# HGRN values of seven heads in token order: blocks by way of memory and VectorE transposes in place of TensorE transposes

## The chip, the core and the metric

The kernel runs on one core of a Trainium2 chip. The core has a matrix engine (TensorE, PE in the profile; its weight loads are PEld), a vector engine (VectorE, DVE), an engine for activations (ScalarE, ACT), GpSimd (POOL) and an engine that here only issues transfers (SyncE, SP). Each of them works through its own queue in order and waits on semaphores for the others; 16 DMA engines move the data. TensorE writes into PSUM, the other tiles lie in SBUF. The metric is the device time of one execution in microseconds (us). The kernel before takes 1769.57 us, the median of three runs (1768.42 to 1771.63).

## The reference, cut to what matters

The program is one step of a decoder layer for 1024 prompt tokens and 8 decode tokens: a norm and one input projection, an HGRN2 recurrence with 8 heads (key and value width 128) beside a Mamba-2 mixer, an output projection, and a gated MLP. The change concerns the HGRN heads, whose core is

```python
def hgrn2_chunk(S, inp):
    q, k, v, g = inp
    b = jnp.cumsum(g, axis=2)
    o = jnp.einsum('bhtk,bhkv->bhtv', q * jnp.exp(b), S)
    decay = jnp.exp(jnp.where(causal, diff, -jnp.inf))
    A = jnp.einsum('bhtsk,bhsk->bhts', decay * q[:, :, :, None, :], k)
    o = o + jnp.einsum('bhts,bhsv->bhtv', A, v)
    S_new = jnp.exp(b_last[:, :, 0])[..., None] * S + jnp.einsum('bhsk,bhsv->bhkv', k * jnp.exp(b_last - b), v)
```

Both products with v sum over the token s. On TensorE the index that is summed lies on the partitions, so v is needed with tokens on the partitions, while the projection leaves it with its 128 channels there.

## The kernel before, in words

**Jobs.** Every large product is cut into jobs; a job (`in_job`, L290) multiplies one 128-column block of a weight with the 1032 tokens in three chunks of 344, with 72 matmuls, and empties each chunk with ScalarE (L819 for the heads). Its weight is loaded by `wload` (L180): a transfer into one of two buffers `ws` (L189), a ScalarE cast into `wh` (L190, two buffers), a VectorE subtraction into `wl` (L192). `load_ahead` keeps the loads two jobs ahead. `head_in` (L807) makes the four jobs of a head: f, q, v and sg. The jobs stand in the order of the Mamba mixer's z0 to z3, head 0's four, z4 to z7, then those of heads 1 to 7, then the output projection. Along with the z jobs runs `ssm_decode` (L627), whose loads (`Bb`, `Cb`, `Sd`) also go through SP and whose arithmetic is on VectorE, ScalarE and GpSimd; each z chunk is gated on VectorE (L673, the tile `sz`), its squares are summed (`gacc`), and matmuls `ms` with the vector work of L651 to L653 and L696 finish the norm during head 0.

**Heads.** `head(h)` (L830) is a generator. `drive` (L266) takes matmuls of the coming jobs between its pieces, in proportion to the numbers that it yields; so head h runs among the matmuls of the jobs of head h+1. It begins when job sg of its own head is done. First come the transposes of the value tile `v`: one for the 8 decode tokens (`vd`, L835) and eight of 128x128 for the prompt (`vtp`, L840), with a ScalarE copy of each four into the half tiles `vt` (L841). Then L902 writes q times f over `v`. The pieces that follow compute the near products (`near`, L882, tiles `a0` to `a6`) between rounds of scaling on VectorE (`scale`, L873 and L874, with the running products `tt` of L879), then the decode states' product (`od`, copied by L944), the transposes of the keys (`ktp`), the state updates (`kv`, L965) and the outputs (`o`), where `kv` and `o` read `vt`. GpSimd's L1003 ends the head and `mix_d` stores it (L1008). The decode values go through memory as well: `vd_d` is written (L844) and read back broadcast as `vb`.

**Order.** PE's order is the program's (`manual_schedule`). The order on the other engines and on SP is set by the framework's scheduler, which places instructions by its own estimates of time; `fetch` (L172) lets a load be placed anywhere behind the last weight load, so that loads can stand ahead of work that the program has earlier.

Of the kernel before, what the change touches and what calls it, by code (L numbers as in the profile page):

```python
# [8 lines left out]
F32 = mybir.dt.float32  # L9
# [7 lines left out]
P = 128  # L17
DM = 1024
T = 1024
# [5 lines left out]
H = 8  # L25
SH = 16
CHUNK = 128
NC = T // CHUNK
# [22 lines left out]
def hybrid_layer(  # L51
# [9 lines left out]
    V, A, G, PE, SP = nc.vector, nc.scalar, nc.gpsimd, nc.tensor, nc.sync  # L61
# [5 lines left out]
    dram = ctx.enter_context(tc.tile_pool(name="dscr", bufs=1, space=DRAM))  # L67
# [3 lines left out]
    def nm(s):  # L71
        cnt[0] += 1
        return f"{s}_{cnt[0]}"
# [8 lines left out]
    def tl(tag, name, dt=F32):  # L82
        w, n = TAGS[tag]
        return (work if tag in ("hT", "big", "e", "g") else tmp).tile([P, w], dt, tag=tag, bufs=n, name=nm(name))

    def half(name):
        return tl("s", name)[:, :512]

    def bank(s, tag="mx"):
        return psmx.tile([P, 512], F32, tag=tag, bufs=NBANK[tag], name=nm(s))  # L90
# [81 lines left out]
    def fetch(dst, src):  # L172

        with tc.issue_after(last_w[0].ins):
            SP.dma_start(dst, src)
# [50 lines left out]
    def job(name, load, run):  # L226
        jobs.append((name, load, run))
# [51 lines left out]
    def w_in(off):  # L279
        return lambda: wload(w_in_[0, :, off:off + P], KT)  # L280

    def steps(w, m0, m1, hi, lo, cs, out):
        kt = len(hi)
        for k in range(kt):
            for i, (a, x) in enumerate(((w[0], hi), (w[0], lo), (w[1], hi))):
                mm(out, a[:, k, m0:m1], x[k][:, cs], start=(k == 0 and i == 0), stop=(k == kt - 1 and i == 2))
                if k < kt - 1 or i < 2:
                    yield True

    def in_job(name, off, evict, begin=None, end=None):  # L290
        def run(w):
            if begin is not None:
                begin()
            for c, cs in enumerate(chunks):
                ps = psmm.tile([P, 512], F32, tag="mm", name=nm("mm"))[:, :CH]
                yield from steps(w, 0, P, hT_hi, hT_lo, cs, ps)
                evict(c, cs, ps)
                if c == NCH - 1 and end is not None:
                    end()
                yield True  # L300
        job(name, w_in(off), run)

    def in_job_last(name, off, evict, begin):

        def run(w):
            begin()
            ps = [psmm.tile([P, 512], F32, tag="mm", name=nm("mm"))[:, :CH] for _ in chunks]
            for k in range(KT):
                for c, cs in enumerate(chunks):
                    for i, (a, x) in enumerate(((w[0], hT_hi), (w[0], hT_lo), (w[1], hT_hi))):  # L310
                        mm(ps[c], a[:, k, :], x[k][:, cs], start=(k == 0 and i == 0), stop=(k == KT - 1 and i == 2))
                        if k < KT - 1 or i < 2:
                            yield True
                    if k == KT - 1:
                        evict(c, cs, ps[c])
                        yield True
        job(name, w_in(off), run)
# [120 lines left out]
    for i in range(9):  # L438
        n = P if i < 8 else ND
# [290 lines left out]
    def once(work):  # L730
        def run():
# [19 lines left out]
    G.affine_select(eye8, eye8, pattern=[[1, ND], [-1, ND]], compare_op=ALU.is_equal, fill=0.0, base=0,  # L751
                    channel_multiplier=0)
    vd_d = dram.tile([H, ND, P], F32, name="vd_d")

    am = const.tile([P, NC, P], F32, name="am")
    G.memset(am, 0.0)
# [50 lines left out]
    def head_in(h):  # L807
        t = {}

        def f_end():  # L810
            f, k = t["f"], tl("big", "k")
            A.activation(f[:, :NT], f[:, :NT], AF.Identity, bias=lbt[:, 0, h:h + 1], scale=lbt[:, 1, h:h + 1])
            V.tensor_scalar(k[:, :NT], f[:, :NT], -1.0, 1.0, op0=ALU.mult, op1=ALU.add)
            t["k"] = k

        for n, off, func in (("f", OFF_F, AF.Sigmoid), ("q", OFF_Q, AF.Silu), ("v", OFF_I, AF.Copy),
                             ("sg", OFF_G, AF.Silu)):
            def evict(c, cs, ps, n=n, func=func):
                A.activation(t[n][:, cs], ps, func)  # L819

            def begin(n=n):
                t[n] = tl("e" if h == 0 and n == "f" else "big", n)

            if h == H - 1 and n == "sg":
                in_job_last(f"{n}{h}", off + h * P, evict, begin)
            else:
                in_job(f"{n}{h}", off + h * P, evict, begin, f_end if n == "f" else None)
        return t

    def head(h, t):  # L830
        f, k, q, v, sg = (t[n] for n in ("f", "k", "q", "v", "sg"))
# [3 lines left out]
        PE.transpose(dps[:ND, :P], v[:, T:NT], ident)  # L835
        vt = [half("vt"), half("vt")]
        for hf in range(2):
            ps = bank("vtp")
            for i in range(4):
                PE.transpose(ps[:, blk[i]], v[:, hf * 512 + i * P:hf * 512 + (i + 1) * P], ident)  # L840
            A.copy(vt[hf], ps)  # L841
# [100 lines left out]
            mm(ops[32 * g:32 * g + 32, :P], qb[:, b, :], Sds[b // 4][:, b % 4, :], start=(b < 4), stop=(b >= 4))  # L942
        odr = small.tile([P, P], F32, tag="odr", bufs=1, name=nm("odr"))
        V.tensor_copy(odr, ops[:, :P])  # L944
        yield 3.5

        for hf in range(2):
# [30 lines left out]
        for hf in range(2):  # L978
            oh = sg[:, hb[hf]]
            ps = bank("o")  # L980
            for i in range(4):
                n = hf * 4 + i
                Sb, c = before[n], slice(n * P, (n + 1) * P)
# [113 lines left out]
    heads = [None] * H  # L1097
    ssm_gate(0)
    heads[0] = head_in(0)
    ssm_gate(1)  # L1100
    heads[1] = head_in(1)
    job("conv", None, once(lambda: spread(conv_states(), 60, lambda: spread(token_blocks(), 40))))
    for h in range(2, H):
        heads[h] = head_in(h)
# [9 lines left out]
    with tc.manual_schedule(engines={mybir.EngineType.PE}):  # L1114
        finish("x3")
        drive(ssd(0), 45.5, "x7")
        drive(ssd(1), 45.5, "v0")
        finish("z7")
        for h in range(H):
            drive(head(h, heads[h]), 32.0 if h else 35.0, f"sg{h + 1}" if h < H - 1 else "o12.2")  # L1120
        finish("o12.6")
        for r0 in (0, 4):
            mixes[r0] = mix_load(r0)
# [321 lines left out]
    for c in (3, 0, 1, 2):  # L1445
# [4 lines left out]
        for t0 in range(cs.start, cs.stop, P):  # L1450
            n = min(P, cs.stop - t0)
# [49 lines left out]
```

## Time and profile before

| | |
|---|---|
| median of three runs | 1769.57 us |
| the profiled execution, and its span | 1770.87 us, 1769.2 us |
| PE busy, DVE busy | 1717.5 us (97%), 1123.7 us (64%) |
| ACT busy, POOL busy | 824.7 us (47%), 503.6 us (28%) |
| matmul of 128x344 in a job | 326 ns long, the next starts 0.16 us later |
| transposes vtp (L840) | x64, 272 ns each; first at 383.4 us, last at 823.1 us |
| first transposes vd (L835) of heads 0 and 7 | 383.3 us, 822.2 us |
| copies of vt (L841) | x16, 598 ns |
| mean DMA rate | 110 GB/s |

The profile is of one execution. A matmul's duration includes the time until its result is out, and the next one starts long before that; what an instruction costs a busy PE is therefore the step from its start to the next start. Rows of waits name the line that waits, the instruction that ended the wait, the total in us, the count and the longest. A timeline row gives start, duration, engine, line and operation, output and inputs, and in brackets the idle time before it with its cause. SPq rows are transfers being issued, not the transfers themselves.

### The profile page before, as it was taken

To read this page: it belongs to the slowest core of one execution; us is meant where nothing else is said; L and a number is where in the kernel's file an instruction comes from. 1 tells how busy PE (TensorE), PEld (TensorE's weight loads), DVE (VectorE), ACT (ScalarE), POOL (GpSimd) and SP (SyncE) were. 2 spreads that over 40 slices of the span, in tenths; PEclk is the share of its full clock that TensorE was granted. 3 is DMA by queue.
4 is the path that set the end of the run, shared out by engine and by line. 5 is a ranking of instruction groups with operands and counts; after the bars stand their busy time and mean duration, and the time that the engine had idled before them with its cause. 6 is when DMAs were issued, how large, how long until landed. Compare 5 with 4: busy or idle time off the path is not lost. (4 is left out here: it accounts for less than half of the span.)

```text
span 1769.2 us, 38520 instructions
## 1 busy us (share of the span) xinstructions
PE 1717.5 (97%) x16079; PEld 1669.4 (94%) x16079; DVE 1123.7 (64%) x2013; ACT 824.7 (47%) x1474; POOL 503.6 (28%) x501
## 2 busy tenths in 40 slices
PE   7999899999999999999899989999999999999998
PEld 6998799989999999999799989999999999999997
DVE  6668967575554565467646677776666667445545
ACT  7577698454545454454423364343333444111114
POOL 2103332120110110112230355766666664000002
PEclk9999999999999999999999999999999999999999
DMA  5355744543221222234336742222222225422212
GB/s 165 66 148 151 188 115 140 179 138 104 76 76 52 85 75 66 71 102 127 113 100 212 244 127 72 72 75 82 96 73 73 73 84 212 151 85 82 97 61 97
DMA packets 247461, 194.95 MB, mean 110 GB/s; under 512 B 46924, under 2 KB 220502, under 8 KB 247270
## 3 DMA queue, kind: packets, MB, share of 16 engines
q1 hardware_dynamic: 246998, 192.38, 36.0%
q8 instruction: 126, 2.06, 0.5%
q14 instruction: 49, 0.40, 0.1%
q0 software_dynamic: 288, 0.10, 0.0%
HBM read 149.92 MB, written 46.91 MB: 111 GB/s over the span
## 5 line engine op out<-in xcount | busy, mean ns | idle before, releaser
L93 PE MATMUL mm<-hh,wh 128*128 128x344 f32 x1248 | 405.7, 326 | 1.6 <-ACT sz L672 1.5
L93 PE MATMUL mm<-hl,wh 128*128 128x344 f32 x1248 | 405.0, 325 | 0.6 <-issue 0.6
L93 PE MATMUL mm<-hh,wl 128*128 128x344 f32 x1248 | 402.2, 323 | 0.0
L93 PEld LDWEIGHTS mm<-hh,wh 128*128 128x128 f32 x1248 | 235.1, 189 | 5.7 <-issue 2.4
L93 PEld LDWEIGHTS mm<-hl,wh 128*128 128x128 f32 x1248 | 235.5, 189 | 3.2 <-issue 1.7
L93 PEld LDWEIGHTS mm<-hh,wl 128*128 128x128 f32 x1248 | 235.6, 189 | 2.1 <-issue 1.4
L190 ACT CAST wh<-ws 128x1024 fp32r<-128x1024 f32 x96 | 100.5, 1047 | 242.5 <-PE dn L93 135.6
L93 PE MATMUL ub<-uh,wh 128*128 128x258 f32 x704 | 199.6, 284 | 0.8 <-DVE fext L1314 0.5
L93 PE MATMUL ub<-ul,wh 128*128 128x258 f32 x704 | 199.3, 283 | 0.0
L93 PE MATMUL ub<-uh,wl 128*128 128x258 f32 x704 | 199.0, 283 | 0.0
L93 PE MATMUL dn<-ah,wh 128*128 128x256 f32 (+1 forms) x640 | 181.2, 283 | 2.0 <-DVE x L1431 2.0
L93 PE MATMUL dn<-al,wh 128*128 128x256 f32 (+1 forms) x640 | 180.5, 282 | 0.0
L93 PE MATMUL dn<-ah,wl 128*128 128x256 f32 (+1 forms) x640 | 180.1, 281 | 0.0
L192 DVE TENSOR_TENSOR wl<-ws,wh 128x1024 fp32r<-128x1024 f32 x88 | 115.0, 1307 | 73.7 <-ACT wh L190 66.9
L93 PE MATMUL mm<-mh,wh 128*128 128x258 f32 x512 | 148.5, 290 | 4.7 <-DVE x L1061 2.9
L93 PE MATMUL ua<-uh,wh 128*128 128x258 f32 x528 | 150.0, 284 | 3.0 <-DVE x L1061 1.8
L93 PE MATMUL ua<-ul,wh 128*128 128x258 f32 x528 | 149.7, 284 | 0.0
L93 PE MATMUL ua<-uh,wl 128*128 128x258 f32 x528 | 148.8, 282 | 0.0
L93 PE MATMUL mm<-ml,wh 128*128 128x258 f32 x512 | 146.7, 286 | 1.7 <-DVE ml L1019 1.7
L93 PE MATMUL mm<-mh,wl 128*128 128x258 f32 x512 | 146.4, 286 | 0.0
L1264 DVE TENSOR_TENSOR wl<-wt,wh 128x512 fp32r<-128x512 f32 x88 | 90.8, 1051 | 75.4 <-ACT wh L1263 75.4
L93 PEld LDWEIGHTS ub<-uh,wh 128*128 128x128 f32 x704 | 133.3, 189 | 1.3 <-DVE fext L1314 0.7
(354 smaller groups left out, 4095.0 us busy)
## 6 DMA issues: line engine op xcount, KB each, us to landing
ws<-in_w_in_dram SPq DMA_DIRECT2D x52, 512.0 KB
ws<-in_w_up_dram SPq DMA_DIRECT2D x44, 512.0 KB
ws<-in_w_out_dram SPq DMA_DIRECT2D x24, 512.0 KB
act_d<-val SPq DMA_DIRECT2D x22, 516.0 KB
al<-act_d SPq DMA_DIRECT2D x22, 516.0 KB
ws<-in_w_down_dram SPq DMA_DIRECT2D x22, 512.0 KB
ml<-mix_d SPq DMA_DIRECT2D x48, 172.0 KB
csb<-cs_d SPq DMA_DIRECT2D x32, 256.0 KB
```

The costliest lines, as they stand in the source:

```text
L93: PE.matmul(out, lhsT, rhs, start=start, stop=stop)
L190: A.copy(wh[:, :n], ws[:, :n])
L192: V.tensor_tensor(wl[:, :n], ws[:, :n], wh[:, :n].bitcast(F32), op=ALU.subtract)
L1264: V.tensor_tensor(lo[:, cs], sums[name], hi[:, cs].bitcast(F32), op=ALU.subtract)
```

## The change

For heads 0 to 6, the eight TensorE transposes and the two ScalarE copies are left out. Instead, when job v of such a head has emptied its last chunk (`v_end`), four transfers write the prompt part of `v` to memory (`vb_d`), one for each 32 partitions, in pieces of 32 tokens (128 B), so that memory holds, for each group of 32 tokens, the 128 channels in one row of 512 B per position in the block. In `head`, eight fetches bring those rows into the two tiles `vt`, 32 partitions at a time, and after the decode product VectorE transposes each tile in place in blocks of 32x32 (`V.transpose`), which puts tokens on the partitions. Head 7 keeps the TensorE transposes. The mathematics is the same.

```diff
+    vb_d = dram.tile([H - 1, 32, NC, 4, P], F32, name="vb_d")
...
+        def v_end():
+            for b in range(4):
+                SP.dma_start(vb_d[h, :, :, :, 32 * b:32 * b + 32].rearrange("j c a r -> j (c a) r"),
+                             t["v"][32 * b:32 * b + 32, :T].rearrange("j (n r) -> j n r", r=32))
+
+        ends = {"f": f_end, "v": v_end if h < H - 1 else None}
...
-                in_job(f"{n}{h}", off + h * P, evict, begin, f_end if n == "f" else None)
+                in_job(f"{n}{h}", off + h * P, evict, begin, ends.get(n))
...
         for hf in range(2):
+            if h < H - 1:
+                for a in range(4):
+                    fetch(vt[hf][32 * a:32 * a + 32].rearrange("j (c n) -> j c n", n=P),
+                          vb_d[h, :, 4 * hf:4 * hf + 4, a, :])
+                continue
             ps = bank("vtp")
...
         V.tensor_copy(odr, ops[:, :P])
+        if h < H - 1:
+            for hf in range(2):
+                V.transpose(vt[hf], vt[hf])
         yield 3.5
```

What the built programs show of the order, at three places. Line numbers behind the change are up to 15 higher. First SP's queue around the start of head 4, before; `ws` are weight loads, `SS` the state of head 3 that is stored, `sg` its result, and `vd` and `vb` the decode values of head 4.

```order
L968 DMA out_dram<-SS_7049 128x128
L189 DMA ws_7514<-in_w_in_dram 128x8x128
L844 DMA vd_d<-vd_7248 8x128
L1008 DMA mix_d<-sg_6334 128x1032
L189 DMA ws_7722<-in_w_in_dram 128x8x128
L175 DMA vb_7253<-vd_d 128x512
L175 DMA vb_7261<-vd_d 128x512
```

The same place in the changed program:

```order
L983 DMA out_dram<-SS_7058 128x128
L819 DMA vb_d<-v_6978 1024x1x32 x4
L189 DMA ws_7523<-in_w_in_dram 128x8x128
L175 DMA vt_7247<-vb_d 32x4x128
L1023 DMA mix_d<-sg_6345 128x1032
L175 DMA vt_7247<-vb_d 32x4x128 x3
L175 DMA vt_7248<-vb_d 32x4x128 x4
L856 DMA vd_d<-vd_7257 8x128
L189 DMA ws_7733<-in_w_in_dram 128x8x128
L175 DMA vb_7262<-vd_d 128x512
L175 DMA vb_7270<-vd_d 128x512
```

The four writes stand ahead of a weight load; one fetch stands ahead of the store of `sg`, seven behind it; and the store of `vd`, which was ahead of that store, is now behind all of these. Second, DVE's queue from the copy of `vd` in head 4, before (twelve rows; `a` are results of PE's near products, `amc` their sum):

```order
L843 COPY vd_7248<-vd_7232 8x128
L192 TENSOR_TENSOR wl_7274<-ws_7272,wh_7273 128x1024
L902 TENSOR_TENSOR v_6969<-q_6761,f_6519 128x1024
L879 TENSOR_TENSOR tt_7268<-f_6519 128x512
L879 TENSOR_TENSOR tt_7269<-tt_7268 128x256
L879 TENSOR_TENSOR tt_7269<-tt_7269 128x128
L879 TENSOR_TENSOR tt_7269<-tt_7269 128x64
L879 TENSOR_TENSOR tt_7269<-tt_7269 128x32
L879 TENSOR_TENSOR tt_7269<-tt_7269 128x16
L879 TENSOR_TENSOR tt_7269<-tt_7269 128x8
L909 TENSOR_TENSOR amc_7270<-a_894_7303,eyec 128x256
L873 TENSOR_TENSOR k_6752<-k_6752,f_6519 128x512
```

In the changed program, a little further on in the same head:

```order
L885 TENSOR_TENSOR f_6526<-k_6759,tt_7277 128x256x2
L886 TENSOR_TENSOR q_6768<-v_6978,tt_7277 128x256x2
L921 TENSOR_TENSOR amc_7279<-a_884_7312,eyec 128x256
L891 TENSOR_TENSOR tt_7278<-tt_7278 128x128
L910 COPY_PREDICATED amc_7279<-mlow,a_885_7313 128x256
L891 TENSOR_TENSOR tt_7278<-tt_7278 128x64
L959 STREAM_TRANSPOSE vt_7247<-vt_7247 128x512
L891 TENSOR_TENSOR tt_7278<-tt_7278 128x32
L959 STREAM_TRANSPOSE vt_7248<-vt_7248 128x512
L891 TENSOR_TENSOR tt_7278<-tt_7278 128x16
L891 TENSOR_TENSOR tt_7278<-tt_7278 128x8
L910 COPY_PREDICATED amc_7279<-mlow,a_888_7434 128x256
```

The multiplication over `v` (L902) now stands directly behind the copy of `vd` and ahead of L192, the two scalings of a round stand ahead of the small products `tt`, and the transposes stand behind the first L898 (here L910), far ahead of the place that the program gives them. Third, head 0: DVE in jobs z6 and z7 of the changed program, where `Bb`, `Cb`, `Sd` and `xdd` belong to the Mamba decode, `gacc` and `xbc` to the gate:

```order
L645 TENSOR_REDUCE xdd_3867<-Cb_3885 128x4
L673 TENSOR_TENSOR xbc_2075<-xbc_2075,sz_3925 128x344
L646 TENSOR_SCALAR xbc_2075<-xbc_2075,d_bc,xdd_3867 128x8
L959 STREAM_TRANSPOSE vt_4121<-vt_4121 128x512
L678 TENSOR_TENSOR gacc_3611<-gacc_3611,sz_3925 128x344
L891 TENSOR_TENSOR tt_4151<-f_3001 128x512
L642 TENSOR_TENSOR Sd_4002<-Sd_4002,Bb_3998 128x512
L641 TENSOR_TENSOR Bb_4013<-Bb_4013,xdd_3996 128x512
```

Before, the rows of L879 (now L891) and L902 of head 0 stood behind the copy of its `vd`, among the norm's L651 to L653:

```order
L843 COPY vd_4130<-vd_4114 8x128
L192 TENSOR_TENSOR wl_4163<-ws_4161,wh_4162 128x1024
L673 TENSOR_TENSOR xbc_2290<-xbc_2290,sz_4109 128x344
L902 TENSOR_TENSOR v_3372<-q_3197,f_3000 128x1024
L879 TENSOR_TENSOR tt_4150<-f_3000 128x512
L651 TENSOR_SCALAR nt_4156<-ms_4154,gacc_3606 128x344
```

They and the transposes of head 0 have moved ahead of it, L902 ahead of the first L673 of job z4. On PE nothing moves: the eight transposes are gone from seven places, and the rest stands in the same order.

## The prediction

> **What bounds the kernel now.** I read the profile page first, for the engine that is always on.
>
> ```profile
> span 1769.2 us, 38520 instructions
> PE 1717.5 (97%) x16079; PEld 1669.4 (94%) x16079; DVE 1123.7 (64%) x2013; ACT 824.7 (47%) x1474; POOL 503.6 (28%) x501
> PEclk9999999999999999999999999999999999999999
> ```
>
> TensorE is busy for 97% of the span. A busy PE can still be one that waits inside its pipeline, so the next view is the table of stretches: PE, DVE and the granted clock around the heads. Head 0 begins at 383 us, the others follow about 61 to 63 us apart, head 7 begins at 822.
>
> ```profile
> 300.00:383.00 83.00, 81.50 (x540) 78.43 (x539) 46.56 (x83) 35.91 (x81) 17.20 (x13) 1.00 0.57 166
> 383.00:452.00 69.00, 64.42 (x819) 61.85 (x818) 44.98 (x80) 40.39 (x61) 6.00 (x5) 0.98 0.29 93
> 640.00:701.00 61.00, 61.00 (x812) 59.43 (x811) 33.45 (x62) 30.64 (x49) 8.47 (x7) 1.00 0.25 72
> 823.00:900.00 77.00, 66.96 (x899) 64.05 (x898) 57.71 (x103) 27.93 (x60) 23.17 (x19) 0.93 0.37 112
> ```
>
> The columns are length, then busy time of PE, PEld, DVE, ACT and POOL, then clock, DMA share and GB/s. In head 4 (640 to 701 us), like in its neighbours, PE has no gap at all and DVE is busy for little over half: there a matmul less is time less. Head 0 is different: 4.6 us of 69 idle, clock 0.98. The view of waits says on whom PE waits there; the first row lies between 300 and 383 us, the next three in head 0, the last after 823 us.
>
> ```profile
> PE mm L93 <- ACT sz L672: 1.5, 1, 1.5
> PE a L93 <- DVE q L874: 2.7, 1, 2.7
> PE ms L93 <- DVE vd L843: 1.5, 1, 1.5
> PE a L93 <- DVE v L874: 0.5, 1, 0.5
> PE xtd L798 <- DVE odr L944: 4.2, 1, 4.2
> ```
>
> So head 0 hangs on VectorE (DVE), which runs the gated norm's products and the head's scalings in one queue. Behind the longest of these waits the clock falls:
>
> ```profile
> 411.50:413.00 1.50, 0.95 (x92) 0.90 (x96) 1.50 (x3) 0.61 (x2) 0.00 (x0) 0.77 0.88 240
> 413.00:415.00 2.00, 2.00 (x68) 1.96 (x54) 1.37 (x4) 0.62 (x1) 0.00 (x0) 0.50 0.29 86
> 415.00:417.00 2.00, 2.00 (x12) 2.00 (x12) 1.50 (x3) 1.42 (x4) 0.00 (x0) 0.82 0.00 0
> ```
>
> The loss against clock 1.00 is 0.23 x 1.5 + 0.50 x 2.0 + 0.18 x 2.0 = 1.7 us.
>
> **Term 1, the transposes that go.** Seven heads lose eight TensorE transposes each. Their price is read from the timeline of PE at the start of head 4:
>
> ```profile
> 639.61 0.27 PE L835 MATMUL vd<-ident,v 128*8 128x128 f32 x1
> 639.72 1.03 PE L840 MATMUL vtp<-ident,v 128*128 128x128 f32 x8
> 640.51 0.40 PE L93 MATMUL mm<-hh,wh 128*128 128x344 f32 x1
> 640.75 0.32 PE L93 MATMUL mm<-hl,wh 128*128 128x344 f32 x1
> 640.91 0.32 PE L93 MATMUL mm<-hh,wl 128*128 128x344 f32 x1
> ```
>
> The eight take the stretch from 639.72 to 640.51, 0.79 us, and the matmul behind them has a step of 0.24 instead of the usual 0.16 us: 0.87 us in all, not eight times the 272 ns that one of them lasts, because they overlap. Heads 1 to 6 are the dense ones: 6 x 0.87 = **5.2 us**, all of it on the path. The 14 ScalarE copies behind them go too; ACT is busy for 30.64 of 61 us in head 4, so I cost them at nothing, as I do the PSUM banks set free.
>
> **Term 2, what replaces them on DVE.** Two 32x32 block transposes per head. The kernel has the same form on its residual input, and the same kinds of transfer:
>
> ```profile
> L794 DVE STREAM_TRANSPOSE xs<-xs x16: 667/708/712, 785.9 to 917.8; 128x512 f32<-128x512 f32 x16
> L175 SPq DMA_DIRECT2D xs<-xb_d x16: 319/323/501, 779.9 to 915.0; - x16
> 30.61 3.40 SPq L775 DMA_DIRECT2D xb_d<-in_x_prompt_dram  x4
> DMA  7656452029981369995239994000000000000000
> DMA packets 4473, 0.78 MB, mean 78 GB/s; under 512 B 4200, under 2 KB 4418, under 8 KB 4470
> ```
>
> 1.4 us of DVE per head. Whether it is hidden, head 4 shows:
>
> ```profile
> 639.92 0.28 DVE L843 COPY vd<-vd 8x128 f32<-8x128 f32 x1 [0.34 <-PE vd L835]
> 640.73 2.35 DVE L192 TENSOR_TENSOR wl<-ws,wh 128x1024 fp32r<-128x1024 f32 x1 [0.53 <-ACT wh L190]
> 643.01 1.21 DVE L902 TENSOR_TENSOR v<-q,f 128x1024 f32<-128x1024 f32 x1
> 644.15 0.68 DVE L879 TENSOR_TENSOR tt<-f 128x512 f32<-128x512 f32 x1
> 644.86 1.65 DVE L879 TENSOR_TENSOR tt<-tt 128x256 f32<-128x256 f32 x6
> 648.90 1.53 DVE L874 TENSOR_TENSOR q<-v,tt 128x512 f32<-128x512 f32 x1
> 652.88 0.45 DVE L898 COPY_PREDICATED amc<-mlow,a 128x256 f32<-128x256 uint8 x1 [2.45 <-PE a L93]
> ```
>
> DVE idles 2.45 us before 652.88, for PE; the two transposes stand just ahead of that place in the new order and take 1.4 of it. Cost **0**. They sit in an in-order queue, though: if the blocks have not landed, the scalings behind them (L873, L874) wait, and PE's near products (the tiles "a") wait for those.
>
> **Term 3, the transfers.** Per head four writes of 1,024 pieces of 128 B and eight fetches, all on SP's queue. The like of the writes, four issues from 30.61 us, took 3.40 us to issue; in that window (30 to 40 us, 0.25 us a digit) the last packets end at 36.25, which is 2.2 us behind the last issue. A fetch issues in 0.32 us. What they meet in head 4:
>
> ```profile
> 624.86 1.22 DVE L192 TENSOR_TENSOR wl<-ws,wh 128x1024 fp32r<-128x1024 f32 x1 [2.68 <-ACT wh L190]
> 626.11 0.37 SPq L189 DMA_DIRECT2D ws<-in_w_in_dram  x1
> 640.23 0.30 SPq L844 DMA_DIRECT2D vd_d<-vd  x1
> 642.03 0.34 SPq L1008 DMA_DIRECT2D mix_d<-sg  x1
> 643.59 1.14 SPq L175 DMA_DIRECT2D vb<-vd_d  x2
> 648.52 1.36 POOL L853 TENSOR_TENSOR vb<-vb,k 128x512 f32<-128x512 f32 x1 [6.52 <-DMA vb<-vd_d]
> 655.05 1.04 ACT L190 CAST wh<-ws 128x1024 fp32r<-128x1024 f32 x1
> 303.08 10.35 SPq L175 DMA_DIRECT2D ecs<-cs_d  x4
> ```
>
> The writes stand ahead of the weight load of 626.11 and put it off by 3.4 us at most. That load fills the buffer which L192 has just released (624.86 + 1.22); the other buffer is cast first, this one at 655.05, 29 us later: cost 0. Seven of the eight fetches stand behind the store of the last head's result, which leaves at 642.03 since it waits for POOL. They issue by 642.4 + 7 x 0.32 = 644.6. The landing I bound by 2.2 us (the writes) and 3.8 us (the vb fetches are out by 644.73, POOL starts on them at 648.52): 646.8 to 648.4. DVE, by its durations in the new order (copy, L902, L192, one L879, four scalings, about 9 us from 639.92), comes to its first transpose near 649. Hidden, with about 1 us to spare and the 1 us of DVE idle that is left behind it. The store of vd, its two broadcasts and the weight load behind them move back by some 4 us; POOL then starts near 652 instead of 648.5, and its result is first needed by the matmuls on the decode state, two phases of PE later: 0.
>
> **Term 4, head 0.** Here the blocks are written at the end of job v0, near 327 us, long before the head. L902 overwrites v and had to wait for PE's transposes; now it waits for the writes alone, and the new order puts it and the L879 products into the z jobs: 1.21 + 0.68 + 1.65 = 3.5 us of DVE work leaves the place where PE waits, and 1.4 us of transposes goes into the z jobs with it. Bounds: all waits between 300 and 452 us and the slow clock vanish, 1.5 + 2.7 + 1.5 + 0.5 + 1.7 = 7.9 us (head 0's own transposes are within it, for PE waits there anyway); or none vanishes and the 3.5 + 1.4 = 4.9 us put in front delay PE in full. DVE is busy for 46.56 of 83 us in the z jobs and its gaps there are waits for the Mamba decode's data, so the row is nearer the first end; PE runs on ScalarE's last free buffer there (the 1.5 us for sz), which keeps me from taking it whole. I take **3.5 us** gained, about half of the good end.
>
> **Sum.** 5.2 + 3.5 = 8.7 us off the profiled execution, which took 1770.87 us (span 1769.2 and 1.7 around it): 1762.2. The median of the three runs, 1769.57, lies 1.3 below that execution, so the forecast for a median is **1760.9 us**. About 0.2% (3.5 us) either way is what a measurement of this kernel can tell from no change.
>
> **The rivals.**
>
> *The blocks land late, and DVE stands at its transposes (slower).* Place: the new instruction behind L898 in heads 1 to 6. For it: the fetches are a burst behind a 516 KB store in one queue, and the row at 303.08 shows four fetches in 10.35 us, 2.6 each. At that price seven are out at 642.4 + 18.1 = 660.5, landed at 664, 14 us after DVE is ready. About 1 us of idle and some 3 us until PE reads the next scalings cover the first 4; 10 us a head stay, and the clock's 1.7: 6 x 11.7 - 8.7 = +61, 1831 us. It decides from about 2 us of stall a head (6 x 2.0 is what 8.7 + 3.5 needs), that is landings after about 656. Against it: the ordinary fetch is out in 0.32 us. [...] The window at 30 us, with 4,200 packets under 512 B, shows four such writes done in under 6 us. [...]
>
> *DVE pays in the z jobs what head 0 gains.* Term 4 is then 0 or a loss of up to 4.9: between 1769.57 - 5.2 = 1764.4 and 1769.3, say 1767. [...]
>
> *The gain is given back after 823 us.* PE idles 10 of 77 us there, 4.2 of it in one wait for DVE. If that chain did not start earlier with the heads, it would take back the 8.7: 1769.6. Against it: its DVE work hangs on head 7's own tiles, which move with PE.
>
> **How the numbers follow.** Forecast 0.58 (1755 to 1764.4), z jobs 0.20, given back 0.07, late blocks 0.15. Faster by over 0.2% is below 1766.0: 0.58 and nearly half of the z jobs' case, 0.09: 0.67. Slower: 0.15 and 0.02 from further slow-clock spells in the z jobs, 0.17. The same: 0.16. The low end is all of terms 1 and 4, 1769.57 - 5.2 - 7.9 = 1756.5, less the 1.2 us by which the fastest run lies under the median: 1755. The high end takes in the z jobs' and the given-back case and the 2 us by which the slowest run lies above: 1771.6. Outside are the late blocks and 0.05.
>
> **What would show it.** Right: L840 with 8 transposes left; heads 1 to 6 each 0.87 us nearer together; 30 block transposes on DVE at about 0.7 us, and no wait of DVE for vt above 1 us; in head 0 the wait for q gone or under 1 us and a clock of 1.00. Wrong: DVE waits for vt, PE waits for L874 in the dense heads, or the wait of 1.5 us for sz grown in the z jobs.

## The result: 2.5 to 4 us faster, where 8.7 were forecast

The median of the changed kernel is 1767.07 us over 19 runs, against 1769.59 us over 19 runs of the kernel before on the same chip: a ratio of 0.9981, 95% interval 0.9975 to 0.9987. A second comparison, on another occasion, gave 0.9978 (0.9968 to 0.9988). Of 1769.6 us that is 3.4 and 3.9 us saved by the ratios, 2.5 by the two medians. The forecast was 1760.9 us, the range 1755.0 to 1771.6. The profiled execution of the changed kernel took 1764.43 us, 2.6 under its median, and the one of before 1.3 over its own, so a difference between these two traces alone (6.4 us) is too large by 3 to 4 us.

The page of the changed kernel, to be held against the first fence of the prediction: the span, TensorE, VectorE, the transfers.

```profile
span 1762.6 us, 38588 instructions
PE 1707.9 (97%) x16023; PEld 1660.7 (94%) x16023; DVE 1148.3 (65%) x2027; ACT 819.3 (46%) x1460; POOL 515.9 (29%) x501
```

TensorE (PE) has 56 instructions fewer, seven times eight, and 9.6 us less busy time; VectorE (DVE) is busy 24.6 us longer. The 14 block transposes are 9.9 us of that; the rest is in instructions that both kernels have and that last longer (q times f is 1.21 us eight times before and 1.21 to 2.32 after), and no view here shows why. The same four stretches as before (length, then busy time of PE, PEld, DVE, ACT and POOL, clock, DMA share, GB/s):

```profile
300.00:383.00 83.00, 80.25 (x530) 77.84 (x526) 52.39 (x91) 37.20 (x82) 16.27 (x13) 1.00 0.66 179
383.00:452.00 69.00, 62.98 (x804) 60.52 (x805) 40.21 (x71) 38.31 (x56) 5.33 (x5) 0.95 0.34 97
640.00:701.00 61.00, 61.00 (x902) 59.21 (x902) 37.96 (x65) 29.55 (x46) 10.22 (x6) 1.00 0.34 92
823.00:900.00 77.00, 66.91 (x788) 64.37 (x787) 52.82 (x95) 26.84 (x58) 22.06 (x20) 0.93 0.36 112
```

The heads begin earlier now, so the stretches don't cover quite the same work. Head 4 is as dense as it was; over the head itself DVE is busy for 36.8 us of 59.9, in place of 33.2 of 60.6, and PE has no gap for it. In head 0 PE is idle for more time than before (6.0 us of 69, was 4.6) and the clock is lower (0.95, was 0.98); the head begins at 380.0 now (383.3 before), so some of its wait lies ahead of this stretch. The waits of PE there:

```profile
PE ms L93 <- DVE vd L855: 6.6, 1, 6.6
PE a L93 <- DVE q L886: 1.7, 1, 1.7
PE a L93 <- DVE v L886: 0.5, 1, 0.5
```

The wait for q fell from 2.7 to 1.7 us and the one for sz in the z jobs is gone, but the gated norm's product ms, which needs the one PSUM bank that vd sits in, now waits 6.6 us (1.5 before) until DVE has copied vd. In the dense heads the change does what it says. The timeline of PE at the start of head 4:

```profile
636.56 0.27 PE L842 MATMUL vd<-ident,v 128*8 128x128 f32 x1
636.58 0.40 PE L93 MATMUL mm<-hh,wh 128*128 128x344 f32 x1
636.82 0.31 PE L93 MATMUL mm<-hl,wh 128*128 128x344 f32 x1
```

From vd to the next matmul it is 0.02 us, where it was 0.90 (639.61 to 640.51): 0.88 us a head. DVE a little later:

```profile
645.38 0.71 DVE L959 STREAM_TRANSPOSE vt<-vt 128x512 f32<-128x512 f32 x1
646.84 0.71 DVE L959 STREAM_TRANSPOSE vt<-vt 128x512 f32<-128x512 f32 x1 [0.68 <-DMA vt<-vb_d]
648.99 0.45 DVE L910 COPY_PREDICATED amc<-mlow,a 128x256 f32<-128x256 uint8 x1 [1.18 <-PE a L93]
```

The second transpose waited 0.68 us for its block, and behind it DVE still waits for PE, 1.18 us. Over all seven heads the view of the tile vt gives, for the transposes and for DVE's waits on the blocks:

```profile
L959 DVE STREAM_TRANSPOSE vt<-vt x14: 699/710/712, 368.3 to 766.5; 128x512 f32<-128x512 f32 x14
  DMA vt<-vb_d: 2.6, 5
```

To see where the time went I take three marks from each trace: the first matmul vd of head 1, that of head 7, and the first matmul n2ms of the second norm. From 440 us on, the rows of vd give the first two (first and last start); of before:

```profile
L835 PE MATMUL vd<-ident,v x7: 270/271/272, 451.8 to 822.2; 128*8 128x128 f32 x7
L93 PE MATMUL n2ms<-n2r,ones x8: 378/381/382, 995.5 to 1060.2; 128*128 128x258 f32 x8
```

and of after:

```profile
L842 PE MATMUL vd<-ident,v x7: 270/271/274, 452.1 to 816.1; 128*8 128x128 f32 x7
L93 PE MATMUL n2ms<-n2r,ones x8: 378/381/382, 989.4 to 1050.5; 128*128 128x258 f32 x8
```

Heads 1 to 6 take 364.0 us in place of 370.4. Up to head 1 nothing is gained, and from head 7 to the second norm the two take the same 173.3 us.

### The profile page after: what moved, and what is told of

It is laid out like the page before. It is cut to its first block, busy times and chain, and to the rows that moved or that the text cites. A ratio compares the mean times of both kernels' runs of the same rounds, so it can differ in the third digit from the quotient of the medians.

```text
span 1762.6 us, 38588 instructions
## 1 busy us (share of the span) xinstructions
PE 1707.9 (97%) x16023; PEld 1660.7 (94%) x16023; DVE 1148.3 (65%) x2027; ACT 819.3 (46%) x1460; POOL 515.9 (29%) x501
## 5 line engine op out<-in xcount | busy, mean ns | idle before, releaser
L192 DVE TENSOR_TENSOR wl<-ws,wh 128x1024 fp32r<-128x1024 f32 x88 | 119.2, 1355 | 70.7 <-ACT wh L190 63.8
```

The costliest lines, as they stand in the source:

```text
L192: V.tensor_tensor(wl[:, :n], ws[:, :n], wh[:, :n].bitcast(F32), op=ALU.subtract)
```

## The experiments

Four theories. **A**: heads 1 to 6 gain as forecast, and head 0 gives part back, because VectorE work moved into the z jobs. **B**: the added load takes back a part in every head. **C**: the time behind head 7 gives the gain back. After the first four kernels below, A's second half split in two: **D** (VectorE's work) and **S** (the transfers on SyncE's queue, SP).

The table is the result in one place. The ratio to the kernel before has its 95% interval; the four columns behind it come from one trace each, read as above: head 1's start, from there to head 7's start, from there to n2ms, and the rest of the span.

| Kernel | ratio (interval) | head 1 at | heads 1-6 | to n2ms | rest |
|---|---|---|---|---|---|
| before (the trace shown) | | 451.8 | 370.4 | 173.3 | 773.7 |
| before against itself | 1.0001 (0.9992, 1.0010) | 451.5 | 370.7 | 172.6 | 773.6 |
| after | 0.9981 (0.9975, 0.9987) | 452.1 | 364.0 | 173.3 | 773.2 |
| after, again | 0.9978 (0.9968, 0.9988) | 452.2 | 364.2 | 174.0 | 772.9 |
| heads 1-6 alone | 0.9977 (0.9967, 0.9987) | 450.7 | 364.2 | 176.1 | 772.9 |
| heads 1-6 alone, again | 0.9973 (0.9962, 0.9984) | 451.5 | 365.2 | 172.9 | 774.0 |
| head 0 alone | 1.0020 (1.0011, 1.0029) | 451.9 | 369.7 | 172.4 | 773.0 |
| after, DVE work of head 0 held | 0.9992 (0.9980, 1.0004) | 454.3 | 364.1 | 176.2 | 773.8 |
| after, vd in another bank | 0.9984 (0.9975, 0.9994) | 450.5 | 364.1 | 173.9 | 771.9 |
| after, head 0's reads late | 0.9986 (0.9975, 0.9997) | 454.5 | 364.1 | 174.2 | 775.1 |
| after, head 0 without transfers | 0.9990 (0.9981, 0.9999) | 450.2 | 365.0 | 173.7 | 775.6 |
| after, head 0's transfers on ScalarE's queue | 0.9991 (0.9981, 1.0000) | 452.8 | 364.3 | 174.7 | 774.3 |
| after, no transfers at all | 0.9979 (0.9970, 0.9989) | 450.8 | 364.7 | 174.8 | 774.0 |
| before + head 0's writes | 1.0021 (1.0010, 1.0031) | 452.9 | 371.2 | 173.5 | 773.6 |
| before + head 0's reads | 1.0005 (0.9994, 1.0017) | 450.1 | 370.9 | 173.3 | 774.5 |
| before + head 0's writes and reads | 1.0012 (1.0004, 1.0020) | 454.4 | 371.2 | 173.2 | 776.2 |
| before + both, twice | 1.0045 (1.0033, 1.0058) | 458.8 | 370.0 | 172.8 | 773.4 |
| after, transposes of heads 1-6 three times | 0.9984 (0.9973, 0.9994) | 454.5 | 364.0 | 175.4 | 774.9 |
| after, transfers of heads 1-6 twice | 1.0079 (1.0059, 1.0098) | 451.9 | 379.3 | 174.5 | 772.2 |
| heads 1-7 | 1.0047 (1.0031, 1.0063) | 452.0 | 364.2 | 188.2 | 774.8 |

The column of heads 1 to 6 repeats to a microsecond: 369.7 to 371.2 without the change there, 364.0 to 365.2 with it. The first column does not repeat so well; five executions in which head 0 is done as before give 450.7 to 452.0, five in which it is done as after 451.9 to 454.5. (Where heads 1 to 6 are changed too, head 1's four writes also stand ahead of its start.) Much of this scatter comes from ahead of the change. Counted from ScalarE's last eviction of job v0 (326.58 us before, 325.09 after), which stands just ahead of the writes, head 1 starts 125.2 to 126.2 us later in the first five, mean 125.7, and 127.0 to 128.6 us later in the second five, mean 127.6. By this measure head 0 costs about 1.9 us.

### Heads 1 to 6 alone, head 0 alone

```
-            if h < H - 1:
+            if 0 < h < H - 1:      # heads 1 to 6; for head 0 alone: if h == 0
```

(at the writes, the reads and the transposes)

> The memory path for heads 1 to 6 alone; head 0 is done on TensorE as in the kernel before. Theory A (heads 1 to 6 gain the eight transposes each, and head 0's work among the last z jobs pays part of it back): the measured change of head intervals, 6.4 us over heads 1 to 6, stays and head 0's loss goes, so 1769.6 - 5.2 to 6.4 = 1763 to 1764.5 us, and no 6.6 us wait of ms for the copy of vd. Theory B (the added load, twelve transfers and two VectorE transposes a head, takes back a part in every head): six sevenths of the 2.5 us gained, 1767.5 us. Theory C (heads 1 to 6 gain 6 us, head 0 nothing, and the time behind head 7 gives most of it back): 1767 us.

> The memory path for head 0 alone; heads 1 to 6 as before. Theory A: slower than before by what separates 2.5 us from 5.2 to 6.4 us, so 1772 to 1773.5 us, with the 6.6 us wait of ms for the copy of vd. Theory B: 1769.2 us. Theory C: 1769.6 us.

Heads 1 to 6 alone saved 4.1 us of 1769.6 (2.3 to 5.8), head 0 alone cost 3.5 us (1.9 to 5.1). B and C wanted head 0 at 1.000 or less: B falls, and C cannot be the whole. A's sizes hold for head 0, though the wait for vd is 4.4 us in that kernel and not 6.6; for heads 1 to 6 its 5.2 to 6.4 lies at the edge of what was measured. The first was measured once more at the end:

> Heads 1 to 6 alone by way of memory, once more, beside the others on one chip. If head 0 costs the changed kernel 1 to 2 us: 0.9970 of before. If it costs nothing: 0.998. In the profile 364.2 us from head 1's start to head 7's, and 947 to 949 us behind it.

It saved 4.8 us (2.8 to 6.7). Against 3.4 and 3.9 for the whole change, head 0 costs about 1 us there, with an uncertainty of some 1.5, and 3.5 us where it is changed alone. These two numbers don't agree well, and no run here settles by how much head 0 pays when the other heads are changed too.

### Is it VectorE's work, or the PSUM bank?

The first kernel queues head 0's product q*f, its products of f and its two transposes behind the copy of vd:

```
-        V.tensor_copy(vd, dps[:ND, :P])
+        cp = V.tensor_copy(vd, dps[:ND, :P])
+        hold = (lambda: tc.issue_after(cp.ins)) if h == 0 else nullcontext
...
+        with hold():
+            V.tensor_tensor(pair[0][1], q[:, :T], f[:, :T], op=ALU.mult)
```

> The changed kernel with head 0's product q*f, its chain of products of f and its two VectorE transposes queued behind head 0's copy of vd on VectorE, so that none of them runs among the z jobs. Theory A: the z jobs and head 0 go as before except for the eight transposes saved, so 1769.6 - 7 x 0.87 = 1763.5 us, at most 2 us more if the held work delays head 0. Theories B and C: 1767 us.

It saved 1.4 us (from 3.5 saved to 0.7 lost), no better than the changed kernel, and its waits of PE in head 0 show the same one (line numbers are one higher here):

```profile
PE ms L94 <- DVE vd L856: 6.2, 1, 6.2
```

None of the moved VectorE work is in front of the copy any more, and the wait is still 6.2 us. The first half of theory A, that this work delays the copy, falls. The second kernel takes the bank away as the cause:

```
-        dps = bank("vd", "nx")
+        dps = bank("vd", "nx" if h else "mx")
```

> The changed kernel with head 0's PSUM tile vd in the pool of four banks, so that ms of the z jobs needs no copy of vd first. Theory A, if the single bank is what turns the late copy into a loss: the 6.6 us wait goes and 3 to 6 us with it, 1761 to 1764 us; if z jobs and head 0 pay the same time at another place (the product a waits for VectorE instead), 1766 to 1767 us. Theories B and C: 1767 us.

2.8 us saved (1.1 to 4.4). The wait for vd is gone, and others have taken most of it over:

```profile
PE a L93 <- DVE q L886: 3.7, 1, 3.7
PE ms L93 <- DVE nt L651: 2.2, 1, 2.2
PE ms L93 <- DVE gacc L678: 0.6, 1, 0.6
```

With the 0.5 us for v that is 7.0 us in place of 8.8. In this one trace head 1 starts 1.6 us earlier than in the changed kernel (450.5), but the ratio is no better, so the bank alone isn't the cause: most of the wait only moved. What lengthens it?

### The transfers of head 0

Two kernels from opposite sides: the kernel before with head 0's four writes and eight reads that serve nothing, and the changed kernel without them (its transposes read the gate sg).

```
+            if h == 0:                       # before + transfers; TensorE path kept behind it
+                for a in range(4):
+                    fetch(vt[hf][32 * a:32 * a + 32]..., vb_d[h, :, 4 * hf:4 * hf + 4, a, :])
```

> The kernel before, with head 0's four writes of v to memory and eight reads into vt added; the TensorE path stays and overwrites vt, so the transfers serve nothing. Theory S (SyncE's queue among the z jobs is what head 0 pays with: Bb, Cb, Sh and the weights are issued later, Sh at 375.3 and 380.0 us in place of 372.2 and 375.4): slower than before by 2 to 4 us, Sh late as in the changed kernel. Theory D (the VectorE work moved into the z jobs is what it pays with): within 1 us of before.

> The changed kernel without head 0's transfers: its two VectorE transposes read the gate sg in place of the fetched blocks, so head 0's values are not those of the reference; heads 1 to 6 as changed. VectorE has the same work as in the changed kernel, with q*f free early. Theory S: head 0 costs nothing, 0.9970 to 0.9960 of before (5 to 7 us gained). Theory D: as the changed kernel, 0.998, with vd copied late and ms waiting for it.

The transfers alone cost 2.1 us (0.7 to 3.5), with head 1 at 454.4, which speaks against D. Without them (the scheduler then puts the two transposes at 399 us, inside head 0, and not among the z jobs) the changed kernel's head 1 starts at 450.2, about 2 us earlier than in the changed kernel, and the wait for vd is 3.0 us:

```profile
PE ms L93 <- DVE vd L855: 3.0, 1, 3.0
```

but its ratio, 0.9990, is not the 0.9960 to 0.9970 that S expected. So S holds on the one side and misses on the other. The next kernel doubles the supposed cause:

> The kernel before with head 0's writes and reads added twice over, serving nothing. Theory S (the transfers among the z jobs delay Bb, Cb, Sh and the weights on SyncE's queue): the 2.1 us that one set cost grow to 4 us or more, 1.0024 or more, head 1 starting at 456 us or later. Theory D (VectorE's order): 0 to 1 us, and what one set showed was chance.

8.0 us lost (5.8 to 10.3), head 1 at 458.8: the cost grows with the transfers, and D falls. It isn't the same wait twice over: the one for vd is 3.9 us, and a new one of 3.4 us, for the weight wl, stands in head 0. Then which of the transfers? One kernel takes head 0's reads out of the z jobs, one adds the writes alone, one the reads alone (from an input tensor, in the same shape).

```
+        if h == 0:                           # reads late: behind the loads of vb
+            with tc.issue_after(ld.ins):
+                ... fetch(vt[hf]..., vb_d[h, ...])
```

> The changed kernel with head 0's eight reads into vt queued on SyncE behind its loads of vb, so only the four writes stay among the z jobs; vt is first needed some 38 us later. Theory S with the reads as its main part: head 0's loss goes, 0.9970 (5 us gained), the wait of ms for the copy of vd gone or under 2 us. Theory S with the writes as its main part, and theory D: as the changed kernel, 0.998.

> The kernel before with head 0's four writes of v to memory added and nothing read back. One set of writes and reads had cost 2.1 us (0.8 to 3.5), two sets 8 us. If the writes are the part that costs (4096 packets of 128 bytes and 2.9 us of SyncE's queue at 325 us, ahead of the loads Bb, Cb and Sd): 1.0010 to 1.0015 of before, head 1 starting near 454 us. If the reads are (eight issues in between Bb, Cb, Sd and Sh): 1.000, head 1 starting at 451 to 452 us.

> The kernel before with head 0's eight reads alone added, of the same shape, from an input tensor into vt (which the TensorE path then overwrites). If the writes are what head 0 pays with (they alone cost 1.0 to 5.5 us): 0.999 to 1.001 of before, head 1 starting at 451 to 452 us. If the reads cost as much: 1.0010 to 1.0020, head 1 starting at 453 us or later.

Late reads changed nothing (0.9986). The writes alone lost 3.7 us (1.8 to 5.5), the reads alone 0.9 (from 1.1 saved to 3.0 lost). These intervals overlap, but the marks agree: from v0's last eviction to head 1 it is 127.9 us with the writes and 124.4 with the reads, against 125.2 to 126.2. So it is the writes, in the main. SP's timeline shows what four writes do (a choice of rows). Before:

```profile
329.57 0.38 SPq L189 DMA_DIRECT2D ws<-in_w_in_dram  x1
331.18 0.50 SPq L175 DMA_DIRECT2D Bb<-bc_d  x1
331.77 0.44 SPq L175 DMA_DIRECT2D Cb<-bc_d  x1
340.05 0.39 SPq L643 DMA_DIRECT2D out_dram<-Sd  x1
343.32 0.37 SPq L189 DMA_DIRECT2D ws<-in_w_in_dram  x1
344.92 0.48 SPq L175 DMA_DIRECT2D Cb<-bc_d  x1
```

With the writes alone added:

```profile
325.44 2.94 SPq L819 DMA_DIRECT2D vb_d<-v  x4
330.29 0.71 SPq L189 DMA_DIRECT2D ws<-in_w_in_dram  x1
331.06 0.96 SPq L175 DMA_DIRECT2D Bb<-bc_d  x1
332.54 1.58 SPq L175 DMA_DIRECT2D Sd<-in_state_ssm_dram  x1
336.88 0.38 SPq L189 DMA_DIRECT2D ws<-in_w_in_dram  x1
345.73 0.38 SPq L643 DMA_DIRECT2D out_dram<-Sd  x1
350.38 0.46 SPq L175 DMA_DIRECT2D Cb<-bc_d  x1
```

Two things changed. For about 6 us behind the writes most issues take 0.7 to 1.6 us in place of 0.4 to 0.5. And the queue's order is another one: the next weight load stands ahead of the Mamba decode's store (336.88, was 343.32), the store leaves at 345.73 (340.05), and the next Cb is asked for at 350.38 (344.92). The decode runs 5 to 6 us later there, and 3 us later by its last store (374.49, was 371.53). The wait of ms for vd is 4.3 us in this kernel, with no other part of the change in it. Most of that growth is not a later copy of vd. Before:

```profile
383.27 0.27 PE L835 MATMUL vd<-ident,v 128*8 128x128 f32 x1
385.56 0.27 DVE L843 COPY vd<-vd 8x128 f32<-8x128 f32 x1
385.88 0.85 PE L93 MATMUL ms<-gacc,ones 128*128 128x344 f32 x2 [1.47 <-DVE vd L843]
384.00:391.00 7.00, 5.53 (x33) 4.89 (x32) 6.22 (x13) 6.34 (x10) 0.00 (x0) 1.00 0.39 113
```

With the writes alone added:

```profile
379.92 0.27 PE L842 MATMUL vd<-ident,v 128*8 128x128 f32 x1
385.00 0.27 DVE L850 COPY vd<-vd 8x128 f32<-8x128 f32 x1
385.33 1.51 PE L93 MATMUL ms<-gacc,ones 128*128 128x344 f32 x2 [4.27 <-DVE vd L850]
384.00:391.00 7.00, 5.67 (x20) 5.20 (x21) 6.22 (x13) 6.23 (x9) 0.00 (x0) 0.57 0.45 127
```

Counted from v0's last eviction (326.58 and 324.97 us), the wait grows by 2.8 us because PE reaches vd 1.7 us earlier (the wait of 1.5 us for sz in the z jobs is gone) and the copy comes 1.0 us later, by no more than it scatters in the five traces with head 0 as before. So most of the wait takes back what PE had gained. Towards its end and behind it the granted clock is low, 0.57 from 384 to 391 us, where it was 1.00; in the changed kernel this stretch has 0.58, without head 0's transfers 0.76. Head 1 starts 2.7 us later by this count: 1.0 for the copy and 1.6 between ms and head 1 (67.6 us in place of 65.9), where the slow clock lies. Whether the 3.7 us of the writes come from the size of their pieces, 128 B, or from the number of them, no run here tells.

One kernel moved head 0's transfers off SP:

```
-                SP.dma_start(vb_d[h, ...
+                (SP if h else A).dma_start(vb_d[h, ...
```

> The changed kernel with head 0's writes and reads issued from ScalarE's queue in place of SyncE's. If the place in SyncE's queue is what head 0 pays with: head 1 starts at 450 to 451 us in place of 452.3, and 0.9965 to 0.9975 of before. If the traffic itself or its bytes in memory are: as the changed kernel, 0.998, head 1 starting at 452 us or later. ScalarE's issues add some 12 x 0.5 us to an engine whose evictions the z jobs wait for, which would show as waits of mm for ACT.

1.6 us saved (0 to 3.4), head 1 at 452.8: not better than the changed kernel. Its wait for vd is down to 1.3 us, and PE waits 3.0 us for ScalarE's sz in the z jobs instead, as the expectation had it for the issues on that engine. Whether the slot in SP's queue, the order that the scheduler gives it, or the traffic is what head 0 pays with stays open.

### The load of heads 1 to 6

```
-                    V.transpose(vt[hf], vt[hf])
+                    for _ in range(3 if h else 1):
+                        V.transpose(vt[hf], vt[hf])
```

> The changed kernel with each VectorE transpose of heads 1 to 6 done three times (three block transposes give the same as one), 2.8 us more VectorE work a head. If VectorE's work is hidden in these heads (the prediction's second term): 59.8 us from head to head, 0.998 of before. If it lies on the path: up to 2.8 us a head, so 1.006 at most.

Four more block transposes a head leave heads 1 to 6 at 364.0 us. Head 4 in that kernel:

```profile
640.00:701.00 61.00, 61.00 (x808) 59.43 (x807) 40.04 (x69) 30.56 (x48) 11.20 (x8) 1.00 0.34 89
```

PE has no gap. DVE's transposes are free there. The transfers:

```
                 SP.dma_start(vb_d[h, ...
+                if h:
+                    SP.dma_start(vb2_d[h, ...
```

(and each read likewise, from vb2_d ahead of vb_d)

> The changed kernel with the transfers of heads 1 to 6 doubled: eight writes into two scratch tensors and sixteen reads a head, the second eight over the first. If the transfers of these heads are hidden (the prediction's third term): 59.8 us from head to head as in the changed kernel, 0.998 of before. If half of what they could gain is paid to SyncE and memory: 0.5 to 1 us more a head, 3 to 6 us slower than the changed kernel. If the blocks come too late with the second reads: a wait of the product kv for VectorE or memory, several us a head.

15 us more for heads 1 to 6 than in the changed kernel, of which about 11.5 lie in head 2 alone (its start to head 3's is 74.0 us, 62.4 in the changed kernel); the others lose 0.3 to 2.0 us each. The waits of PE and of DVE in head 2, and the stretch:

```profile
PE a L93 <- DVE v L921: 3.2, 1, 3.2
PE cst L333 <- DMA rt<-in_state_conv_ffn_dram: 2.1, 1, 2.1
DVE vt L966 <- DMA vt<-vb_d: 5.6, 1, 5.6
516.00:588.00 72.00, 64.82 (x806) 61.80 (x806) 39.60 (x73) 28.19 (x44) 9.89 (x7) 0.93 0.38 92
```

DVE stands 5.6 us at the transpose because the blocks have not landed; the product q*f (L921), now further back in DVE's order, keeps PE 3.2 us; a load of another stage is late in the same queue; and the clock falls to 0.93. One set of transfers is hidden in these heads, two are not in head 2: this is the rival of late blocks, at twice the traffic and clearly in one head of six.

### What happens behind head 7

> The kernel before against itself, for what one more profiled execution of it shows: 1.000, head 1 starting at 451 to 452 us, 370.5 us from head 1's start to head 7's, and 945 to 950 us behind head 7's start.

> The changed kernel itself once more, beside the other three on one chip: 0.998 of before, the wait of ms for the copy of vd at 6 to 7 us if the program's own order makes it, and near 1.5 us if it was one execution's chance.

> The changed kernel without any of the transfers: the VectorE transposes of heads 0 to 6 read the gate sg, so these heads' values are not those of the reference. If all that the change could gain is lost to transfers: 0.9960 of before (7 us). If the time behind head 7's start gives back part of what the heads gain (rival 3): 364 us from head 1's start to head 7's, but 0.998 of before, with over 948 us behind head 7's start.

The kernel before against itself shows no difference, and its trace repeats the marks. The changed kernel's second trace has the wait of ms for vd at 4.4 us, between what the two readings expected: it is the program's, and its length varies. Without any transfer the kernel saved 3.7 us (1.9 to 5.3), no more than the changed one: what caps the gain is not the transfers of the seven heads. Rival 3's numbers hold: 364.7 us for heads 1 to 6, and 948.8 us behind head 7's start. From head 7 to n2ms the seven traces without a change in heads 1 to 6 take 172.4 to 173.5 us, mean 173.0; the eleven with it (heads 1-7 and the doubled transfers left out) 172.9 to 176.2, mean 174.5. About 1.5 us of what the heads gain is given back there, by these means; the changed kernel's own two traces have 173.3 and 174.0. Behind n2ms the means are 774.0 and 773.9. The last kernel asked whether a gain in head 7 itself would stay:

```
-            if h < H - 1:
+            if h:
```

> Head 0 on TensorE and heads 1 to 7 by way of memory. If head 7 gains as heads 1 to 6 do and nothing more is given back behind it: 0.9970 of before, 1 us under the variant with heads 1 to 6. If the time between head 7's start and the second norm is set by ScalarE and VectorE evictions and transfers, so that a gain there is given back: as the variant with heads 1 to 6, 0.9975, with that stretch at 174 us or more less 0.9.

It lost 8.3 us (5.5 to 11.1): the stretch from head 7 to n2ms takes 188.2 us, some 14 more than in the other kernels, against the 6 that heads 1 to 6 gain. Its waits of PE and of ScalarE, and the stretch:

```profile
PE mm L93 <- ACT mh L1033: 12.1, 4, 4.5
ACT mh L1033 <- DMA ml<-mix_d: 13.7, 7, 6.1
818.00:840.00 22.00, 10.04 (x156) 7.86 (x157) 13.16 (x29) 7.45 (x19) 0.00 (x0) 0.53 0.77 249
```

In head 7 the output projection reads the heads' results back (ml), in the queue that now also carries vt. PE waits 12.1 us in four pieces and works at a clock of 0.53 for 22 us. So head 7 hangs on these transfers, and whether a gain there would stay is not answered: the cost came first.

No kernel here is clearly better than the changed one; heads 1 to 6 alone (0.9977 and 0.9973) is the best by a margin inside the intervals.

## Why the prediction was right and wrong

**Term 1, the transposes (5.2 us): right, a little small.** The step of 0.87 us measured 0.88. Heads 1 to 6 gain 370.6 - 364.35 = 6.2 us in the means of the table's traces. Six times 0.88 is 5.3; most of the other 0.9 lies in head 3 (61.5 to 59.8 us), where the kernel before had a gap: of before, and of after in its second trace,

```profile
578.00:640.00 62.00, 61.44 (x813) 59.54 (x812) 33.10 (x63) 30.77 (x49) 8.80 (x7) 1.00 0.24 71
```

```profile
578.00:640.00 62.00, 62.00 (x815) 60.46 (x814) 38.35 (x66) 31.12 (x48) 12.52 (x7) 1.00 0.34 88
```

The view of waits names no engine for that gap (0.6 us, "issue"), and what closed it stays open.

**Term 2, VectorE in the heads (0): right**, shown by the threefold transposes. (DVE's time in head 4 grew by 3.6 us and not by 1.4, and that is hidden too.) On which of the two engines a transpose costs less, the row decides here: TensorE has no gap, and VectorE has 21 of 61 us free even with the threefold transposes.

**Term 3, the transfers (0): right in heads 1 to 6, and not asked where it mattered.** Its margin was not. The landing in head 4 was put at 646.8 to 648.4 us, 7.2 to 8.8 us behind the matmul vd, ahead of DVE, which was to come 9.4 us behind it. DVE came 8.8 us behind vd (645.38, vd at 636.56) and the second half's blocks 10.3 us (646.84), so DVE waited 0.68 us where 1 us was to spare; DVE's idle time behind it hid that. The rival of late blocks did not come; its chance of 0.15 was the author's estimate, and no run here shows what the size of the pieces costs apart from their number. But the writes were costed only ahead of the weight load at 626.11, with 29 us to spare. The same four writes at the end of job v0 stand in front of the decode's loads, which have no such slack.

**Term 4, head 0 (3.5 us gained): wrong, this is the step that failed.** It failed in two places. The first is the gain. "3.5 us of DVE work leaves the place where PE waits" did happen, and the wait for q shrank by 1.0 us; that half of the waits and of the slow clock would go with it did not. In the two kernels without head 0's transfers, where no write can be the reason, PE's waits between 290 and 456 us are 6.5 and 5.2 us, against 6.2 before, because the wait for vd grew (3.0 and 2.5 us, was 1.5). From v0's last eviction to head 1 these kernels take 124.9 and 125.0 us, against a mean of 125.7 before: 0.7 us, no more than head 0's own eight transposes. (Their transposes stand at 398 and 399 us, so VectorE's order is not quite that of the changed kernel.) The second is the price of the writes among the z jobs, which the term put at nothing: alone they cost 3.7 us. In place of a gain of 3.5, head 0 costs 1 us (whole change against heads 1 to 6 alone) to 3.5 us (head 0 alone). The bad end of its bounds had the right sign, with 4.9 us, and the wrong cause: not VectorE's work, which could be held back without changing the wait. The rival "DVE pays in the z jobs what head 0 gains" gave 1767 and the median is 1767.07; its number came out by luck, for its mechanism did not.

**Given back behind 823 us (0.07): in part.** About 1.5 us, in the stretch up to the second norm. The argument against it, that this work hangs on head 7's own tiles, left out the transfers and evictions of the output projection that share that stretch; which of them takes the 1.5 us back, no run here shows.

**The sum.** -6.2 in heads 1 to 6, +1 to +1.9 up to head 1, +1.5 behind head 7: 2.8 to 3.7 us gained, against 3.4 and 3.9 by the two ratios. The forecast's base was sound: 1769.57 for three runs, 1769.59 for 19.

## What to carry to other kernels

A step that is moved has to be costed at each place where it will stand: the writes were free in heads with slack in the queue (heads 1 to 6 took 364.0 us with all transfers, 364.7 without any) and cost 3.7 us where a chain of loads stood behind them, and the dense heads, where the profile was easiest to read, said nothing about that place. A shorter wait on one engine is not a gain until the order of the other queues has been read too; here the wait was for a copy on VectorE, what lengthened it came through SyncE's queue, and giving the tile another bank mostly renamed the wait. A longer wait also need not mean that what is waited for comes later: here, in the greater part, PE came earlier. Stage marks compared over several traces (heads 1 to 6 repeat to a microsecond) tell where a 0.2% change goes better than the medians or any single trace does.

## What was not expected of the hardware

A burst of writes slowed the issues behind it: after 4 x 1,024 pieces of 128 B most of the next transfers took 0.7 to 1.6 us to issue in place of 0.4 to 0.5, for about 6 us.

The granted clock stayed low longer than the waits lasted. In the kernel with heads 1 to 7 changed, with 12.1 us of waits in four pieces, the longest 4.5 us, the clock was 0.53 over 22 us. In head 0 of the kernel before it fell behind a wait of 2.7 us, to 0.50 from 413 to 415 us; in the changed kernel the same product waited 1.7 us and the clock behind it stayed at 1.00 (413 to 419 us). How long a wait has to be to lower it, no run here shows.
